# Twelve modulation chunks of the second layer computed by VectorE instead of TensorE

## The chip, the cores and the metric

The kernel runs on one core of a Trainium2 chip. The metric is the device time of one execution in microseconds (us); the time given for a kernel is the median of several runs. One more execution is recorded by the hardware profiler, and all rows of the trace come from it.

## The reference, cut to what matters

Two transformer blocks follow each other. The first has two layers on 256 context and 256 latent tokens; each layer scales and shifts its normalised input by six vectors of 1024 that come from one small condition, and ends in a gated feed-forward with a short convolution. The second block has two layers of its own and is not touched.

```python
mod_l = split(silu(c)     @ ada_w[l] + ada_b[l], 6)   # latent tokens
mod_c = split(silu(c_ctx) @ ada_w[l] + ada_b[l], 6)   # context tokens
hl = rms_norm(x_lat, norm_g[l, 0]) * (1 + mod_l[1]) + mod_l[0]
x_lat = x_lat + mod_l[2] * (mix_l @ w_out[l])
x_lat = x_lat + mod_l[5] * conv_ffn(modulate(x_lat, norm_g[l, 1], mod_l[3], mod_l[4]), ...)
```

The matrix `ada_w[l]` is 1024 x 6144 for each of two layers, and its product has only two rows (latent and context). It is handled in chunks of 256 columns: four chunks for each of the six vectors (types 0 to 5), 48 chunks in all.

## The kernel before, in words

Weights are streamed from HBM in blocks of 128 x 2048 floats (1 MB), in the order that `_plan` writes out. `wraw` issues each load on SP's queue into one of two `raw` buffers. A weight block is then split by `split` (lines 394 to 406) into two halves of 1024 columns, and each half into a high part (`whi`, a rounding copy on ScalarE, L401) and a low part (`wlo`, a subtraction on VectorE, L405). TensorE multiplies high by high, high by low and low by high (L444 to L446 in `mm_t`), so 48 matmuls of 512 columns make one block for 512 tokens.

A modulation chunk is another kind of entry in the same plan. It is not split: `ada` (line 534) multiplies the raw block with the activated condition `sc` in eight matmuls of 32 weight columns and 256 moving columns (L539; the trace shows 16 records for one chunk), ScalarE copies the result out (L545), and later, deferred by a cost, two transposes (L549), a reduction (L551) and an addition (L554) on VectorE put it into `mod`. The helper `spread` sets chunks between the weight blocks, one behind each, and keeps as many at the end as its third argument says.

The first feed-forward stage, `_ffn` with l = 0, runs over all 512 tokens in six parts of the hidden width. `up(i)` makes 22 blocks in all, gates and values: each result goes from PSUM through a convolution (ScalarE L1292, VectorE L1295 and L1296), a gate (L1304 to L1306) and a split of its own (L645, L649). `down(i - 1)` follows `up(i)` and adds 11 blocks into the stream `xt` (L1337). The results rotate through five PSUM buffers in this stage (`g` and `s`). The last `down` carries the normalisation of the next layer with it; then `flush_ada` handles chunks that stand at the end of the stage in the plan.

The order of the instructions on each engine is made by a scheduler of the framework, from the order in which the program writes them and from when their inputs and buffers come free. `_Pipe.tick` is called behind each group of matmuls with its cost and spaces out work that is interleaved, in units of columns times passes: a weight block of 48 matmuls of 512 columns counts 24576.

Of the kernel before, what the change touches and what calls it, by code (L numbers as in the profile page):

```python
# [10 lines left out]
F32 = mybir.dt.float32  # L11
F32R = mybir.dt.float32r
BF16 = mybir.dt.bfloat16
AF = mybir.ActivationFunctionType
ALU = mybir.AluOpType
# [13 lines left out]
C_ADAB = 0  # L29
C_NG = C_ADAB + 96  # L30
# [33 lines left out]
T_MB0 = 5440  # L64
T_MB1 = 5568
T_N = 5824

PERM = [16 * c + 4 * b + a for a in range(4) for b in range(4) for c in range(16)]

# [56 lines left out]
def _plan():  # L126
    p = []

    def cols(name, c0, cn=256, k0=0, kn=8, kind="g", at=0):
        p.append((kind, name, k0, kn, c0, cn, at))  # L130

    def ada(l, j, c):
        cols(("ada_w", l), 1024 * j + 256 * c, kind=("a", l, j, c))

    def adas(l, js):
        return [(l, j, c) for j in js for c in range(4)]

    def wout(l, half):
        for n in range(2):
            cols(("w_out", l), 512 * n, 512, 4 * half, 4, at=W_T if l else 0)  # L140

    def up(l, f0, fn):
        for s in range(fn // 2):
            cols(("ffn_up", l), 128 * f0 + 256 * s, at=W_T if l else 0)
            cols(("ffn_up", l), DFF + 128 * f0 + 256 * s, at=W_T if l else 0)

    def down(l, f0, fn):
        if fn == 4:
            cols(("ffn_down", l), 0, 512, f0, 4, at=W_T if l else 0)
            cols(("ffn_down", l), 512, 512, f0, 4, at=W_T if l else 0)  # L150
        else:
            cols(("ffn_down", l), 0, 1024, f0, 2, at=W_T if l else 0)

    def ffn(l):
        for i, fp in enumerate(FPARTS):
            up(l, *fp)
            if i:
                down(l, *FPARTS[i - 1])
        down(l, *FPARTS[-1])

    def spread(extra, start, tail=0, skip=0):
        q = list(extra)
        body = p[start:]
        del p[start:]
        for i, x in enumerate(body):
            p.append(x)
            if i >= skip and len(q) > tail:
                ada(*q.pop(0))
        while q:
            ada(*q.pop(0))  # L170

    e = ("even_w_in", 0)
    for c in range(4):
        if c == 3:
            cols(e, 512, 512, 4, 4)
        ada(0, 1, c)
        ada(0, 0, c)
        if c == 0:
            cols(e, 512, 512, 0, 4)
    n = len(p)  # L180
    for c0 in (2576, 2064, 2320, 0, 256, 1024, 1280):
        cols(e, c0, at=0 if c0 < 1024 else W_N)
    spread(adas(0, (2, 4)), n)
    n = len(p)
    cols(e, 1536)
    cols(e, 1792)
    wout(0, 1)
    wout(0, 0)
    a3, a5 = adas(0, (3,)), adas(0, (5,))
    spread(a3 + a5[:2], n, 1)  # L190
    n = len(p)
    late = adas(1, (2, 4, 3, 5))
    ffn(0)
    spread(a5[2:] + adas(1, (1, 0)) + late[:9], n, 1)
    o = ("odd_w_in", 0)
    n = len(p)
    for c0 in (512, 0, 256, 1280, 768, 1792, 1536, 1024, 2048):
        cols(o, c0, at=W_N)
    wout(1, 0)
    wout(1, 1)  # L200
    spread(late[9:16 - 1], n, 1, 3)
    n = len(p)
    ffn(1)
    spread(late[16 - 1:], n)
    a = ("a_w_in_2", 0)
    for hg in range(4):
        for g in range(3):
            for s in range(3):
                cols(a, 3072 * g + 1024 * s + 256 * hg, at=W_N)
        cols(a, 9216 + 256 * hg, at=W_T)  # L210
    for half in range(2):
        for n in range(2):
            cols(("a_w_out_2", 0), 512 * n, 512, 4 * half, 4, at=W_T)
    cols(("ple_w_proj_2", 0), 0, 1024, 0, 2, at=W_T)
    for n in range(4):
        cols(("ple_w_gate_2", 0), 256 * n, at=W_T)
    b = ("b_w_in_2", 0)
    cols(b, 1024, at=W_N)
    for hg in range(4):
        cols(b, 256 * hg, at=W_N)  # L220
        cols(b, 1280 + 256 * hg, at=W_T)
    for half in range(2):
        for n in range(2):
            cols(("b_w_out_2", 0), 512 * n, 512, 4 * half, 4, at=W_T)
    cols(("ple_w_proj_2", 1), 0, 1024, 0, 2, at=W_T)
    for n in range(4):
        cols(("ple_w_gate_2", 1), 256 * n, at=W_T)
    return p
# [8 lines left out]
class _Pipe:  # L237
    def __init__(self):
        self.pending, self.live = [], []
        self.pace = 1e9  # L240
        self.credit = 0.0
        self.later = []

    def defer(self, cost, fn):
        self.later.append([cost, fn])
# [26 lines left out]
            self.live.append(u)  # L272

    def tick(self, cost):
        if not self.pending and not self.live:
            return
        self.credit += cost
        if self.credit >= self.pace:
            self.credit = min(self.credit - self.pace, self.pace)
            self.slot()  # L280
# [29 lines left out]
class _K:  # L310
# [222 lines left out]
    def ada(self, kind, raw, now=False):  # L533
        nc = self.nc
        _, l, j, c = kind
        acc = self.po(128, 256) if now else self.pg(128, 256)
        for k in range(KD):
            g = 32 * (k % 4)
            nc.tensor.matmul(acc[g:g + 32], self.sc[:, k, :], raw[:, k], start=(k < 4), stop=(k >= 4))  # L539
        self.pipe.tick(2048)  # L540
        sb = self.e(256)
        if self.ada_vec:
            nc.vector.tensor_copy(sb, acc)
        else:
            nc.scalar.copy(sb, acc)  # L545
        def fin():
            tp = self.pt(128, 2, 128)
            for q in range(2):
                nc.tensor.transpose(tp[:, q], sb[:, 128 * q:128 * q + 128], self.ident)  # L549
            red = self.small([128, 2, 2], "adr")  # L550
            nc.vector.tensor_reduce(red, tp.rearrange("p q (g m) -> p q m g", g=4)[:, :, 0:2, :], axis=AX.X, op=ALU.add)  # L551
            o = self.mod[l][:, j, :, 2 * c:2 * c + 2].rearrange("p t q -> p q t")
            a0 = C_ADAB + 48 * l + 8 * j + 2 * c
            nc.vector.tensor_tensor(o, red, self.cols[:, a0:a0 + 2].unsqueeze(2).to_broadcast([128, 2, 2]), op=ALU.add)  # L554
            if j in (1, 4):
                g = C_NG + 16 * l + 8 * (j // 3) + 2 * c
                nc.vector.scalar_tensor_tensor(o, o, 1.0, self.cols[:, g:g + 2].unsqueeze(2).to_broadcast([128, 2, 2]),
                                               op0=ALU.add, op1=ALU.mult)

        if now:  # L560
            fin()
        else:
            self.pipe.defer(6000, fin)

    def stat(self, n):
        return [self.sa.tile([128, n], F32, tag=f"st{n}", name=self.nm("st")), n, 0]
# [707 lines left out]
def _ffn(K, l, segs, st, nxt=None):  # L1274
    nc, tc, cols = K.nc, K.tc, K.cols
    t0, n = segs[0][0], segs[-1][1] - segs[0][0]
    ns = n // 256
    with tc.tile_pool(name=f"f{l}", bufs=1, reuse_waits="tile") as pool, tc.tile_pool(name=f"fw{l}", bufs=3, reuse_waits="tile") as wx:
# [66 lines left out]
                         K.norm(st[0], l + 1, 0, segs[1], 256, 3) if st else ())  # L1345

        K.wide = True
        for i in range(len(FPARTS)):
            up(i)
            if i:  # L1350
                down(i - 1)
        K.lookahead = 0
        K.wide = False
        nst = nxt(segs) if nxt else None
# [596 lines left out]
def _layout(i):  # L1951
# [28 lines left out]
            w[n, :, 1024 * x:1024 * x + 1024] = src.reshape(ka, 128, cb).transpose(1, 0, 2).reshape(128, 1024)  # L1980
    out["w"] = w
    out["tab"] = _tables()
    return out


# [15 lines left out]
```

## Time and profile before

| | us |
|---|---|
| median of 3 runs | 1638.07 (1638.04 to 1639.7) |
| profiled execution, its own time | 1643.18 |
| span of the profiled execution | 1641.4 |
| TensorE busy (matmul) in the span | 1566.8 |
| VectorE busy | 1123.0 |
| ScalarE busy | 776.4 |
| GpSimd busy | 267.0 |

The span runs from the first to the last recorded instruction. PE is TensorE's matmul row, PEld its weight loads, DVE is VectorE, ACT is ScalarE, POOL is GpSimd, SP issues most of the loads. A wait is put down to the event that came last.

### The profile page before, as it was taken

How to read it: one execution, taken by the hardware profiler on the slowest of the kernel's cores; microseconds unless marked ns; L12 is line 12 of the kernel's file. 1: busy time of each engine (PE TensorE's matmuls, PEld its weight loads, DVE VectorE, ACT ScalarE, POOL GpSimd, SP SyncE). 2: the span in 40 equal slices, each digit the busy share in tenths (PEclk: the TensorE clock that was granted, in tenths of full speed). 3: DMA queues.
4: the chain of work that ended last, by engine and by line, in shares of the span. 5: the costliest groups of instructions: out<-in, count | busy, mean ns of one | idle time of the engine just before them, and what ended most of it. 6: DMA issues, size and time to landing. Idle time of an engine off the chain costs nothing.

```text
span 1641.4 us, 28309 instructions
## 1 busy us (share of the span) xinstructions
PE 1566.8 (95%) x11390; PEld 1374.0 (84%) x11390; DVE 1123.0 (68%) x2173; ACT 776.4 (47%) x1422; POOL 267.0 (16%) x239
## 2 busy tenths in 40 slices
PE   5989989999999999998999989999999999999998
PEld 3777767877777788878888889999989999989887
DVE  3676556675655566577677788677676767678896
ACT  3445464353333334234555465554455555455554
POOL 2321100030000000014231344441010101020111
PEclk9999999999999999999999999999999999999999
DMA  8232243344554532231333455554524343516232
GB/s 345 99 111 100 81 155 103 129 154 154 176 183 154 191 121 99 103 109 60 121 111 121 154 200 186 180 198 149 184 102 159 107 174 106 177 59 220 103 126 82
DMA packets 45107, 231.74 MB, mean 141 GB/s; under 512 B 12740, under 2 KB 15940, under 8 KB 18224
## 3 DMA queue, kind: packets, MB, share of 16 engines
q1 hardware_dynamic: 43776, 227.76, 40.0%
q10 hardware_dynamic: 1200, 2.17, 0.5%
q8 instruction: 90, 1.47, 0.4%
q14 instruction: 41, 0.34, 0.1%
HBM read 228.79 MB, written 1.12 MB: 140 GB/s over the span
## 4 chain that ended last, share of the span: by engine, by line
PE 75%; DVE 10%; POOL 4%; ACT 3%; DMA 2%; issue 2%; POOLq 0%; ACTq 0%; DVEq 0%; SPq 0%
PE g L444 10%; PE g L445 10%; PE g L446 10%; PE g L489 6%; PE g L491 6%; PE g L490 6%; PE s L444 4%; PE s L446 4%; PE s L445 4%; DVE wlo L405 3%; PE o L1049 3%; DMA raw<-in_w_dram 2%; PE t L1039 2%; PE g L539 2%; PE s L912 1%
## 5 line engine op out<-in xcount | busy, mean ns | idle before, releaser
L405 DVE TENSOR_TENSOR wlo<-raw,whi 128x1024 fp32r<-128x1024 f32 x289 | 358.6, 1252 | 180.6 <-ACT whi L401 179.9
L401 ACT CAST whi<-raw 128x1024 fp32r<-128x1024 f32 x322 | 332.6, 1048 | 312.4 <-DMA raw<-in_w_dram 123.7
L489 PE MATMUL g<-whi,H 128*128 128x256 f32 x1040 | 299.3, 288 | 4.3 <-ACT H L638 2.6
L491 PE MATMUL g<-whi,H 128*128 128x256 f32 x1040 | 295.7, 285 | 2.0 <-DVE H L640 1.0
L490 PE MATMUL g<-wlo,H 128*128 128x256 f32 x1040 | 293.8, 283 | 0.0
L444 PE MATMUL g<-H,whi 128*128 128x256 f32 (+1 forms) x872 | 274.0, 318 | 5.7 <-ACT H L1649 2.8
L445 PE MATMUL g<-H,whi 128*128 128x256 f32 (+1 forms) x872 | 273.3, 315 | 1.3 <-DVE H L1651 0.6
L446 PE MATMUL g<-H,wlo 128*128 128x256 f32 (+1 forms) x872 | 271.2, 312 | 0.0
L489 PEld LDWEIGHTS g<-whi,H 128*128 128x128 f32 x1040 | 198.5, 191 | 11.8 <-issue 4.6
L491 PEld LDWEIGHTS g<-whi,H 128*128 128x128 f32 x1040 | 198.1, 191 | 4.7 <-DVE H L640 3.0
L490 PEld LDWEIGHTS g<-wlo,H 128*128 128x128 f32 x1040 | 198.4, 191 | 0.5 <-issue 0.2
L444 PEld LDWEIGHTS g<-H,whi 128*128 128x128 f32 x872 | 163.7, 189 | 22.1 <-ACT H L1649 3.2
L445 PEld LDWEIGHTS g<-H,whi 128*128 128x128 f32 x872 | 164.9, 189 | 14.7 <-DVE H L640 1.8
L446 PEld LDWEIGHTS g<-H,wlo 128*128 128x128 f32 x872 | 165.0, 189 | 9.6
L1013 POOL TENSOR_SCALAR P<-P,rc 128x512 f32<-128x512 f32 (+2 forms) x64 | 54.6, 854 | 492.4 <-DVE rc L1811 258.7
L403 POOL TENSOR_TENSOR wlo<-raw,whi 128x1024 fp32r<-128x1024 f32 x33 | 81.1, 2457 | 105.7 <-ACT whi L401 104.5
L446 PE MATMUL s<-H,wlo 128*128 128x256 f32 (+1 forms) x264 | 88.1, 334 | 1.8 <-DVE wlo L405 1.8
L444 PE MATMUL s<-H,whi 128*128 128x256 f32 (+1 forms) x264 | 89.3, 338 | 0.0
L445 PE MATMUL s<-H,whi 128*128 128x256 f32 (+1 forms) x264 | 87.9, 333 | 0.0
L444 PE MATMUL g<-G,whi 128*128 128x256 f32 (+1 forms) x240 | 79.1, 330 | 2.1 <-DVE e L1296 2.1
L446 PE MATMUL g<-G,wlo 128*128 128x256 f32 (+1 forms) x240 | 78.1, 326 | 0.0
L445 PE MATMUL g<-G,whi 128*128 128x256 f32 (+1 forms) x240 | 78.1, 325 | 0.0
(420 smaller groups left out, 3047.6 us busy)
## 6 DMA issues: line engine op xcount, KB each, us to landing
raw<-in_w_dram SPq DMA_DIRECT2D x209, 1024.0 KB, 4.8
xt<-in_xt_dram SPq DMA_DIRECT2D x4, 512.0 KB, 5.4
mrow<-Md ACTq DMA_DIRECT2D x8, 256.0 KB, 4.7
nab<-in_rpb_dram SPq DMA_DIRECT2D x16, 128.0 KB, 3.6
out_dram<-xt SPq DMA_DIRECT2D x4, 256.0 KB, 4.5
agw<-in_agw_dram SPq DMA_DIRECT2D x1, 512.0 KB, 13.8
mka<-in_tab_dram SPq DMA_DIRECT2D x1, 512.0 KB, 3.4
plr<-in_p_dram SPq DMA_DIRECT2D x2, 256.0 KB, 3.6
```

The costliest lines, as they stand in the source:

```text
L401: nc.scalar.copy(hi, raw)
L403: nc.gpsimd.tensor_tensor(lo, raw, hi.bitcast(F32), op=ALU.subtract)
L405: nc.vector.tensor_sub(lo, raw, hi.bitcast(F32))
L444: nc.tensor.matmul(out, hi[:, k, s], X[0][:, x], start=f, stop=False)
L445: nc.tensor.matmul(out, hi[:, k, s], X[1][:, x], start=False, stop=False)
L446: nc.tensor.matmul(out, lo[:, k, s], X[0][:, x], start=False, stop=l)
L489: nc.tensor.matmul(out, X[0][:, a + k, s], hi[:, k], start=f, stop=False)
L490: nc.tensor.matmul(out, X[0][:, a + k, s], lo[:, k], start=False, stop=False)
L491: nc.tensor.matmul(out, X[1][:, a + k, s], hi[:, k], start=False, stop=l)
L539: nc.tensor.matmul(acc[g:g + 32], self.sc[:, k, :], raw[:, k], start=(k < 4), stop=(k >= 4))
L1013: nc.gpsimd.tensor_scalar(P[1], P[1], rc[:, 1:2], 0.0, op0=ALU.mult, op1=ALU.add)
L1049: nc.tensor.matmul(o[64 * e:64 * e + 64], vv(e, b), u["T"][e][:, b], start=(b == 0), stop=(b == kb - 1))
```

## The change

Twelve chunks of layer 1 (types 1, 0 and 2, four each) leave the plan, and with it the stream of raw blocks. `vector_ada` computes them instead: the activated condition of both token kinds is spread over all partitions (`cb`, 128 x 2 x 1024), and a chunk of `ada_w`, transposed on the host (`v`), comes as two loads of 128 x 1024 in three buffers `ar`. For each of the 24 half chunks and each token kind, one `tensor_tensor_reduce` multiplies a row of weights by the condition and sums it, with the bias as the start value, straight into `mod`. The steps are taken from `tick`, one for each 15000 units of cost, in the stage `_ffn` with l = 0; what is left is done ahead of the last `down`. The order of the chunks that stay is changed so that seven of them stand behind the first seven weight blocks of the stage and none at its end.

```diff
+VECTOR = [(1, j, c) for j in (1, 0, 2) for c in range(4)]
+VPACE = 15000
@@ _plan
-    late = adas(1, (2, 4, 3, 5))
+    late = adas(1, (4, 3, 5))
     ffn(0)
-    spread(a5[2:] + adas(1, (1, 0)) + late[:9], n, 1)
+    spread(a5[2:] + late[:5], n)
...
-    spread(late[9:16 - 1], n, 1, 3)
+    spread(late[5:11], n, 1, 3)
     n = len(p)
     ffn(1)
-    spread(late[16 - 1:], n)
+    spread(late[11:], n)
@@ _Pipe
+        self.side = None
...
     def tick(self, cost):
+        if self.side:
+            self.side(cost)
@@ _K
+    def vector_ada(self, pool):
+
+        nc = self.nc
+        cb = pool.tile([128, 2, 1024], F32, name="cb")
+        nc.sync.dma_start(cb.rearrange("p t k -> p (t k)"), self.aps["cb"].partition_broadcast(128))
+        jobs = [(l, j, 2 * c + q, n, q) for n, (l, j, c) in enumerate(VECTOR) for q in range(2)]
+
+        def fetch(i):
+            t = pool.tile([128, 1024], F32, tag="ar", name=self.nm("ar"), bufs=3)
+            nc.sync.dma_start(t, self.aps["v"][jobs[i][3]][:, 1024 * jobs[i][4]:1024 * jobs[i][4] + 1024])
+            return t
+
+        tiles = [fetch(0), fetch(1)]
+        yield
+        for t in range(2):
+            for s in (slice(0, 512), slice(512, 1024)):
+                sg = self.e(512)
+                nc.scalar.activation(sg, cb[:, t, s], AF.Tanh, scale=0.5)
+                nc.vector.tensor_scalar(sg, sg, 0.5, 0.5, op0=ALU.mult, op1=ALU.add)
+                nc.vector.tensor_mul(cb[:, t, s], cb[:, t, s], sg)
+            yield
+        for i, (l, j, m, _, _) in enumerate(jobs):
+            raw = tiles.pop(0)
+            if i + 2 < len(jobs):
+                tiles.append(fetch(i + 2))
+            a0 = C_ADAB + 48 * l + 8 * j + m
+            out = self.mod[l][:, j, :, m:m + 1]
+            for t in range(2):
+                prod = raw if t else pool.tile([128, 1024], F32, tag="prod", name=self.nm("prod"), bufs=1)
+                nc.vector.tensor_tensor_reduce(prod, raw, cb[:, t], 1.0, self.cols[:, a0:a0 + 1], ALU.mult, ALU.add,
+                                               out[:, t])
+                if t and j in (1, 4):
+                    g = C_NG + 16 * l + 8 * (j // 3) + m
+                    nc.vector.tensor_scalar(out, out, 1.0, self.cols[:, g:g + 1], op0=ALU.add, op1=ALU.mult)
+                yield
+
+    def side_step(self, steps):
+        state = [0.0]
+
+        def step(cost):
+            state[0] += cost
+            if state[0] >= VPACE:
+                state[0] -= VPACE
+                next(steps, None)
+
+        return step
@@ _ffn
         K.wide = True
+        steps = None
+        if split:
+            steps = K.vector_ada(pool)
+            next(steps)
+            K.pipe.side = K.side_step(steps)
         for i in range(len(FPARTS)):
             up(i)
             if i:
                 down(i - 1)
+        K.pipe.side = None
+        for _ in steps or ():
+            pass
@@ _layout (host)
+    out["cb"] = np.concatenate([i["c"][0], i["c_ctx"]])
+    out["v"] = np.stack([...])
```

## Rows read from the trace of the kernel before

**Rows 1.** The page: busy time by engine, and the chain that ended last.
```profile
PE 1566.8 (95%) x11390; PEld 1374.0 (84%) x11390; DVE 1123.0 (68%) x2173; ACT 776.4 (47%) x1422; POOL 267.0 (16%) x239
...
PE 75%; DVE 10%; POOL 4%; ACT 3%; DMA 2%; issue 2%; POOLq 0%; ACTq 0%; DVEq 0%; SPq 0%
```

**Rows 2.** Windows: stretch, length, busy us (instructions) by engine, clock, DMA share, GB/s.
```profile
345.00:728.00 383.00, 382.60 (x1946) 306.04 (x1944) 236.96 (x386) 138.82 (x192) 5.97 (x9) 1.00 0.42 144
360.00:560.00 200.00, 200.00 (x1065) 153.66 (x1064) 114.72 (x188) 70.36 (x98) 0.00 (x0) 1.00 0.49 169
600.00:700.00 100.00, 100.00 (x443) 82.81 (x442) 60.09 (x84) 34.07 (x42) 0.00 (x0) 1.00 0.28 95
```

**Rows 3.** Windows, instructions of L539 alone, then of L549: matmuls, weight loads.
```profile
360.00:560.00 200.00, 17.13 (x256) 6.67 (x256) 1.00 0.49 169
...
360.00:560.00 200.00, 6.08 (x32) 4.43 (x32) 1.00 0.49 169
```

**Rows 4.** Timeline of TensorE around one chunk: start us, duration, line, operation.
```profile
449.43 0.39 PE L446 MATMUL s<-G,wlo 128*128 128x512 f32 x1
449.75 1.07 PE L539 MATMUL s<-raw,sc 128*32 128x256 f32 x16
450.75 0.50 PE L444 MATMUL g<-G,whi 128*128 128x512 f32 x1
```

**Rows 5.** Waits of TensorE's weight loads, 353 to 728 us: total, times, longest.
```profile
PEld g L444 <- ACT e L1292: 2.9, 7, 0.4
```

**Rows 6.** Timeline of TensorE where the stage ends; idle time before in brackets.
```profile
728.09 1.07 PE L539 MATMUL g<-raw,sc 128*32 128x256 f32 x16
...
731.74 0.39 PE L489 MATMUL g<-whi,H 128*128 128x256 f32 x1 [2.58 <-ACT H L638]
```

**Rows 7.** Windows behind the end of the stage; the third number from the right is the granted clock.
```profile
738.00:743.00 5.00, 5.00 (x25) 5.00 (x25) 2.57 (x12) 0.41 (x1) 1.17 (x3) 0.51 0.01 3
```

**Rows 8.** Groups of VectorE, 360 to 700 us: count, busy us, mean ns, idle before.
```profile
L405 DVE TENSOR_TENSOR wlo<-raw,whi 128x1024 fp32r<-128x1024 f32 x61 | 73.2, 1222 | 50.6 <-ACT whi L401 50.5
...
L1306 DVE TENSOR_TENSOR e<-e,e 128x512 f32<-128x512 f32 x22 | 15.2, 690 | 0.6
...
L1305 DVE SCALAR_TENSOR_TENSOR e<-e,e 128x512 f32<-128x512 f32 x22 | 15.0, 682 | 0.0
...
L1295 DVE SCALAR_TENSOR_TENSOR e<-g,hw,e 128x510 f32<-128x510 f32 x14 | 10.5, 747 | 7.6 <-ACT e L1292 7.6
...
L551 DVE TENSOR_REDUCE adr<-t 128x4 f32<-128x16 f32 x17 | 3.0, 174 | 17.9 <-PE t L549 17.5
L554 DVE TENSOR_TENSOR mod<-adr,cols 128x4 f32<-128x4 f32 x17 | 2.8, 164 | 0.4
```

**Rows 9.** Instructions of L1808, a `tensor_tensor_reduce` elsewhere: ns min/median/max, first and last start.
```profile
L1808 DVE CUSTOM_DVE_ANT_0 e<-s,mka x32: 674/686/693, 1193.7 to 1440.2; 128x512 f32<-128x512 f32 x32
L1808 DVE DVE_READ_ACCUMULATOR2_ANT nb<- x32: 77/83/85, 1194.3 to 1440.9; 128x1 f32 x32
```

**Rows 10.** Timelines of SP, ScalarE and TensorE early in the stage; then ScalarE later.
```profile
364.08 0.33 SPq L391 DMA_DIRECT2D raw<-in_w_dram  x1
...
368.98 2.00 ACT L401 CAST whi<-raw 128x1024 fp32r<-128x1024 f32 x2 [1.11 <-DMA raw<-in_w_dram]
...
376.35 0.50 PE L444 MATMUL g<-H,whi 128*128 128x512 f32 x1
...
628.03 1.06 ACT L401 CAST whi<-raw 128x1024 fp32r<-128x1024 f32 x1 [1.20 <-PE s L445]
```

**Rows 11.** Loads from 0 to 40 us (GB/s in slices, then one group), then from 280 to 400.
```profile
GB/s 0 8 91 305 356 221 340 369 352 385 414 422 410 418 442 442 401 406 447 438 414 434 426 442 401 442 426 442 164 41 8 164 393 434 401 434 434 311 434 385
...
raw<-in_w_dram SPq DMA_DIRECT2D x11, 1024.0 KB, 10.4
...
raw<-in_w_dram SPq DMA_DIRECT2D x16, 1024.0 KB, 4.9
```

**Rows 12.** Timelines of SP and ScalarE at the start of the stage.
```profile
332.88 0.33 SPq L391 DMA_DIRECT2D raw<-in_w_dram  x1
...
339.09 1.99 ACT L401 CAST whi<-raw 128x1024 fp32r<-128x1024 f32 x2
...
343.54 0.60 ACT L638 ACTIVATE H<-e,mod 128x256 fp32r<-128x256 f32 x1 [2.46 <-DVE e L632]
```

More of the change, by code (lines that the diff above doesn't have):

```diff
@@ L1982, in _layout @@
     out["tab"] = _tables()
+    out["cb"] = np.concatenate([i["c"][0], i["c_ctx"]])
+    out["v"] = np.stack([i["ada_w"][l][:, 1024 * j + 256 * c:1024 * j + 256 * c + 256].T.reshape(2, 128, 1024)
+                         .transpose(1, 0, 2).reshape(128, 2048) for l, j, c in VECTOR])
     return out
```

## The prediction

> **What bounds the kernel now.** I read the busy shares first, then the chain that ended last [rows 1]. TensorE is busy for 95% of the span and holds 75% of the chain, VectorE 10%. So time is saved where TensorE gets less to do, provided that nothing else comes late there. An average over the span doesn't say that for the stage that is changed, so the second view is the busy time by stretch [rows 2]: from 345 to 728 us, which is the first feed-forward stage, TensorE has 382.6 of 383 us and granted clock 1.00, VectorE 237.0, and GpSimd nearly nothing. A busy matmul row alone proves little, because the shown durations overlap. The count does: between 600 and 700 us, where no modulation chunk runs, 442 weight loads and their matmuls pass, one every 0.2262 us, and TensorE has no idle time. The waits of TensorE in the stage are a few microseconds in all, in pieces of 0.4 us [rows 5]. TensorE sets this stage, and the removed work lies in it.
>
> **What is removed from TensorE.** The plan of before has 19 chunks in this stage: 2 of layer 0, 16 of 1 (the three types that are moved, and type 4) and one of type 3. Eighteen stand between the 33 weight chunks, the last one behind the last down projection. The new plan leaves 7, all between the first weight chunks. So 11 vanish from the dense stretch and one from the end of the stage.
>
> Price of one chunk in the dense stretch, two ways. Between 360 and 560 us there are 1064 weight loads [rows 2]; 256 belong to chunks (16 records each, so 16 chunks) and 32 to their transposes [rows 3]. The other 776 at 0.2262 us make 175.5 us; the remaining 24.5 us over 16 chunks are 1.53 us each. Directly, the matmul before a chunk starts at 449.43 us and the one behind it at 450.75 [rows 4]: 1.32 us, less one matmul's 0.23, is 1.09 us, without the transposes that come later. I take 1.5, because the count holds everything that a chunk costs; the direct row is the lower bound. 11 x 1.5 = 16.5 us less (12.0 to 16.8).
>
> The twelfth chunk, at 728.09 us, lies where TensorE has nothing else: it ends at 729.16 and the next layer's first matmul starts at 731.74, held by the normalisation on VectorE and ScalarE [rows 6]. Without it TensorE idles 1.1 us longer and saves nothing. What could change is the clock: from 738 to 743 us it is granted at 0.51, so about 1.2 GHz, after that idle time [rows 7]. The longer pause can move that stretch. All 5 us at the lower level cost some 2.5 us over the higher one, so the bounds are +2.5 (as much again at the lower clock) and -1.5 (the chunk's own time after all); I take 0, since the pause is there already.
>
> **What is added to VectorE.** 12 chunks become 24 jobs of two multiply-and-sum instructions, 48 on 128x1024. No row shows that form with two inputs in SBUF. The nearest are the subtraction of 128x1024 at 1.222 us [rows 8] and the same instruction on 128x512 with one input in PSUM, 0.686 us and 0.083 us for reading the sum [rows 9]; a plain product of 128x512 takes 0.690 [rows 8], so the sum costs little. 48 x (1.222 + 0.083) = 62.6 us. The table of the activated condition adds 8 operations of 128x512, under 0.69 each: 5.5 us. The 12 old reductions and additions, 0.174 + 0.164 us [rows 8], go: 4.1 us less. Net +64 us, on 237 in a stage of some 367: 82% busy. The cover is VectorE's idle time, 40 of 100 us even in the densest stretch of up and down projections [rows 2]. An evacuation can stand behind one of the new instructions for 1.3 us; a chunk's accumulators are five PSUM buffers deep, and an up chunk fills two in 10.9 us, so I price it at 0, and at +3 if the cover is patchy. ScalarE loses 12 copies and gains four Tanh; it was busy for a third of the stage.
>
> The Trainium skill has a rule against this: "Vector Engine (DVE) Microarchitecture Reference", section 7, says that the scalar-tensor-tensor form with two SBUF sources that aren't bf16 runs at half throughput, since both read ports are taken and none is left for the accumulator. The trace doesn't bear it out for the plain form: the gating product with two fp32 sources takes 0.682 us for 512 elements against 0.690 for a plain product [rows 8]. With an accumulator no run here shows it. What it would do is the second rival.
>
> **Queues that the change is moved past.** The 24 loads of 512 KB and the 1 MB table go on SP's queue, in order with the weights. The bytes of the chunks are the same 12 MB as before. A load waits for its buffer, that is for the second product of the job three before it, and the weights behind it on SP wait too. How much they can wait is different in two parts of the stage. Where no chunks run, ScalarE splits a weight half when TensorE frees a buffer (628.03 us, released by a matmul), not when a load lands [rows 10]: weights are several half chunks ahead. Where chunks run, the two raw buffers are held by them: a weight load is issued at 364.08, its first split starts on landing at 368.98 and is over at about 371.2 with VectorE's part, and TensorE wants it at 376.35 [rows 10]. The slack is some 5 us. After the change that part is 7 chunks long instead of 18, and a 512 KB load in front costs it 1.2 to 2.5 us (half of the 2.4 at 434 GB/s, and half of 4.9) [rows 11]: within the slack, 0.
>
> At the entry three loads, 2 MB, go in front of the first weights. Alone a megabyte lands in 4.9 us; in the full queue of the kernel's start, in 10.4 [rows 11]. So the load issued at 332.88 us, whose split starts at 339.09, may be 5 to 10 us late, and behind that split on ScalarE stands the normalisation at 343.54 that feeds TensorE [rows 12]. The split takes 2 us, so it has 2.5 us of room: 0 to 8 us are lost, I take 2, as TensorE waits for the normalisation there anyway.
>
> **Sum.** -16.5 + 0 (end) + 0 (VectorE) + 0 (queue) + 2 (entry) = -14.5 us. The profiled execution took 1643.2 us (span 1641.4), 5.1 over the median of the three timed runs, 1638.07; none of the terms depends on that difference. 1643.2 - 14.5 = 1628.7 for a profiled run, and 1638.07 - 14.5 = 1623.5 for the median. The bounds: -16.8 - 1.5 = -18.3 gives 1619.8; -12 + 2.5 + 3 + 8 = +1.5 gives 1639.6 if everything goes badly together; the entry and VectorE alone at their bad ends, -16.5 + 8 + 3 = -5.5, give 1632.6.
>
> **Rivals.**
> *First: the weights stand behind VectorE in SP's queue (slower).* Place: the 7 chunks at the start of the stage, where the slack is 5 us. The new steps are 15000 cost units apart, against 24576 for a weight chunk of 10.9 us: one step each 6.7 us. If a load stands in SP's queue ahead of weights and its buffer comes free only one step later, the weights start 6.7 us late and 1.2 to 2.5 behind the transfer: 8 to 9 us, 3 to 4 beyond the slack, for each of 7 weight chunks, 21 to 28 us. Taking 24: 1638.07 - 14.5 + 24 = 1647.5. It decides once the delay is over 5 us. Against it: order on the queues follows readiness (weights are split several chunks early today), and VectorE has idle time for the products.
>
> *Second: the sum halves VectorE's rate.* The products take 2.45 us: 48 x 2.53 = 121 us, VectorE 354 of 367 us. Two up chunks, 21.8 us, hold 4 splits (4.9), 8 taps of the convolution (6.0) and 6 operations of gating and its low part (4.1), 15.0 us [rows 8], plus 3.3 products (one a step of 6.7 us), 8.3 us: 23.3, over TensorE's 21.8. Eleven such pairs give back 16.5 us: 1623.5 + 16.5 = 1640, no measurable change.
>
> *Third: the chunks were no load.* If the pieces of 0.4 us around them were all that TensorE could do anyway, for example because the evacuations set the pace, the stage stays as long: 1638. Against it: the matmul period is the same with and without chunks.
>
> **How the numbers follow.** The sum with its bounds gets 0.73, the first rival 0.11, the second 0.08, the third 0.08. Faster by over 0.2% (3.3 us, about what a measurement of this kernel can tell from no change): the forecast's 0.73 and a little of the second, 0.75; within 0.2%: the third, most of the second and the forecast's worst corner, 0.13; slower: the first and what of the second goes further, 0.12. The range, 1617.5 to 1638.5, takes 2 us below the best sum for order that shifts elsewhere, and above reaches just past the third rival, so that the second's and the first's 0.19 are left out.
>
> **What would show it.** Right: 12 groups of 16 narrow matmuls missing, the last weight chunk of the stage starting some 14 us earlier, TensorE at 0.226 us per matmul throughout, VectorE near 80% with products at 1.2 to 1.3 us. First rival: TensorE idle between 345 and 440 us, released by splits, and SP waiting for products. Second: products over 2 us and TensorE waiting for evacuations. Entry: a gap before 360 us and the table's landing time. Wrong altogether: no idle time in the stage, and time lost in a stage that the change does not touch.

## The result, and the profile after

The changed kernel takes 1623.66 us (1620.44 to 1626.03), the kernel before 1638.48 beside it (1638.04 to 1639.7). The ratio is 0.9899, with an interval of 0.9886 to 0.9912, so 14.4 to 18.7 us less; the two medians alone differ by 14.8 us, the ratio stands for 16.5. The forecast was 1623.5. The profiled execution of after took 1623.34 us (span 1621.6), that of before 1643.18, so this pair differs by 19.8 us. Executions of one program scatter by several us (before ran from 1635 to 1645 us in the comparisons below), so the readings that follow compare the stage itself and not the spans.

The page of after, busy time by engine, then the chain that ended last, then the new loads (KB each, us from issue to landing); it answers to [rows 1]:

```profile
PE 1548.0 (95%) x11174; PEld 1366.0 (84%) x11174; DVE 1173.7 (72%) x2257; ACT 774.9 (48%) x1414; POOL 266.6 (16%) x239
...
PE 74%; DVE 10%; ACT 4%; POOL 3%; DMA 3%; issue 2%; POOLq 0%; ACTq 0%; DVEq 0%; SPq 0%
...
ar<-in_v_dram SPq DMA_DIRECT2D x24, 512.0 KB, 4.5
...
cb<-in_cb_dram SPq DMA_DIRECT2D x1, 1024.0 KB, 5.5
```

TensorE has 18.8 us less busy time and VectorE 50.7 more, and yet the shares of the chain hardly move: TensorE still sets the time. Where the time went is seen by stage. From the first matmul of the feed-forward stage to the first matmul of the next layer, before takes 332.96 to 731.74 us, which is 398.78, and after 332.30 to 715.16, which is 382.86: 15.9 us less. The two first matmuls of the stage, before and then after:

```profile
332.96 0.50 PE L444 MATMUL g<-H,whi 128*128 128x256 f32 x2
...
332.30 0.50 PE L450 MATMUL g<-H,whi 128*128 128x256 f32 x2
```

The next layer and its feed-forward stage are 391.66 and 388.64 us long, the second block 518.0 and 517.8. The 3.0 us in the next layer are no more than one code scatters there from trace to trace (386.4 to 390.4 us in this kernel and the four runs below with the same code in that layer and no chunk at the end of the stage). So the gain that stands clear of scatter lies in the stage that was changed.

Windows of after through that stage, as in [rows 2] (stretch, length, then busy us and instructions of PE, PEld, DVE, ACT, POOL, granted clock, DMA share, GB/s):

```profile
345.00:360.00 15.00, 14.82 (x82) 12.54 (x81) 14.08 (x27) 9.28 (x15) 4.33 (x5) 1.00 0.41 156
360.00:400.00 40.00, 40.00 (x223) 30.05 (x222) 38.80 (x71) 17.53 (x25) 0.00 (x0) 1.00 0.68 237
400.00:440.00 40.00, 39.47 (x195) 30.25 (x194) 38.18 (x64) 16.90 (x24) 0.00 (x0) 1.00 0.75 264
440.00:480.00 40.00, 40.00 (x178) 33.12 (x177) 39.43 (x60) 14.20 (x17) 0.00 (x0) 1.00 0.59 200
480.00:520.00 40.00, 40.00 (x178) 33.13 (x177) 39.77 (x64) 15.88 (x20) 0.00 (x0) 1.00 0.43 154
520.00:560.00 40.00, 40.00 (x178) 33.13 (x177) 25.42 (x34) 13.82 (x17) 0.00 (x0) 1.00 0.31 105
560.00:700.00 140.00, 140.00 (x626) 116.22 (x625) 84.00 (x126) 44.09 (x55) 0.00 (x0) 1.00 0.30 99
```

Read the DVE column first. From 360 to 520 us VectorE is busy for 156.2 of 160 us, 98%, where before it had 115 of 200 [rows 2]; behind 520 us it falls back to 60%. The new work was not spread over the stage at 82%, as its pacing by cost would have it: it was done at the first chance. Then the PE column: TensorE loses 0.5 us in the slice from 400 to 440 us and nothing afterwards. From 440 us on, 177 weight loads pass in each 40 us, one every 0.226 us, the same as in the stretch of before without chunks.

The instructions of the tile `ar` (ns min/median/max, first and last start):

```profile
L600 DVE CUSTOM_DVE_ANT_0 prod<-ar,cb,cols x24: 1270/1278/1284, 357.6 to 521.0; 128x1024 f32<-128x1024 f32 x24
```

VectorE's groups from 345 to 714 us (count, busy us, mean ns, idle before), as in [rows 8]:

```profile
L411 DVE TENSOR_TENSOR wlo<-raw,whi 128x1024 fp32r<-128x1024 f32 x68 | 82.7, 1220 | 35.5 <-ACT whi L407 35.4
...
L600 DVE DVE_READ_ACCUMULATOR2_ANT mod<- 128x1 f32 x48 | 3.9, 81 | 0.0
```

One product has a record of 1.278 us, and reading its sum one of 0.081. Records of neighbours overlap, so these two don't simply add. VectorE's timeline (start, duration):

```profile
392.95 1.28 DVE L600 CUSTOM_DVE_ANT_0 prod<-ar,cb,cols 128x1024 f32<-128x1024 f32 x1
394.16 0.08 DVE L600 DVE_READ_ACCUMULATOR2_ANT mod<- 128x1 f32 x1
394.16 0.68 DVE L702 TENSOR_TENSOR G<-e,G 128x512 fp32r<-128x512 f32 x1
```

The next instruction starts 1.21 us after the product did, together with the read of the sum. Where VectorE doesn't wait, this distance is 1.20 to 1.33 us, mostly 1.2, so the 48 take some 58 us, between 357.6 and 524 us.

What TensorE waits for from 353 to 712 us (total, times, longest), and what SP's queue waits for from 330 to 540:

```profile
PEld g L452 <- DVE wlo L411: 1.3, 3, 0.5
...
SPq L397 <- DVE wlo L411: 89.1, 17, 13.0
SPq L580 <- DVE mod L600: 56.2, 18, 8.2
```

SP does stand behind the products: 18 waits, up to 8.2 us. TensorE's weight loads wait 1.3 us in all for low parts. The first rival's queue is there, and its cost isn't.

### The profile page after: what moved, and what is told of

It is laid out like the page before. It is cut to its first block, busy times and chain, and to the rows that moved or that the text cites. A ratio compares the mean times of both kernels' runs of the same rounds, so it can differ in the third digit from the quotient of the medians.

```text
span 1621.6 us, 27974 instructions
## 1 busy us (share of the span) xinstructions
PE 1548.0 (95%) x11174; PEld 1366.0 (84%) x11174; DVE 1173.7 (72%) x2257; ACT 774.9 (48%) x1414; POOL 266.6 (16%) x239
## 4 chain that ended last, share of the span: by engine, by line
PE 74%; DVE 10%; ACT 4%; POOL 3%; DMA 3%; issue 2%; POOLq 0%; ACTq 0%; DVEq 0%; SPq 0%
PE g L450 10%; PE g L452 10%; PE g L451 10%; PE g L495 6%; PE g L497 6%; PE g L496 6%; PE s L450 4%; PE s L451 4%; PE s L452 4%; DVE wlo L411 3%; PE o L1102 3%; DMA raw<-in_w_dram 2%; PE t L1092 2%; PE g L545 1%; PE s L965 1%
## 5 line engine op out<-in xcount | busy, mean ns | idle before, releaser
L450 PE MATMUL g<-H,whi 128*128 128x256 f32 (+1 forms) x856 | 267.2, 315 | 5.1 <-ACT H L1710 2.7
L451 PE MATMUL g<-H,whi 128*128 128x256 f32 (+1 forms) x856 | 266.7, 313 | 1.0 <-DVE H L1712 0.3
L452 PE MATMUL g<-H,wlo 128*128 128x256 f32 (+1 forms) x856 | 264.9, 311 | 2.4 <-DVE wlo L411 2.4
L450 PEld LDWEIGHTS g<-H,whi 128*128 128x128 f32 x856 | 161.0, 189 | 19.1 <-ACT H L1710 3.1
L451 PEld LDWEIGHTS g<-H,whi 128*128 128x128 f32 x856 | 161.7, 189 | 13.1 <-DVE H L693 1.5
L450 PE MATMUL s<-H,whi 128*128 128x512 f32 (+1 forms) x280 | 95.1, 340 | 1.1 <-ACT H L691 1.1
L451 PE MATMUL s<-H,whi 128*128 128x512 f32 (+1 forms) x280 | 94.9, 339 | 0.0
L452 PE MATMUL s<-H,wlo 128*128 128x512 f32 (+1 forms) x280 | 94.3, 337 | 0.0
```

The costliest lines, as they stand in the source:

```text
L450: nc.tensor.matmul(out, hi[:, k, s], X[0][:, x], start=f, stop=False)
L451: nc.tensor.matmul(out, hi[:, k, s], X[1][:, x], start=False, stop=False)
L452: nc.tensor.matmul(out, lo[:, k, s], X[0][:, x], start=False, stop=l)
```

## The experiments

The theory: TensorE sets the stage, a chunk among the weights costs it 1.5 us, and VectorE's added work and loads are covered as long as the weights have a lead. Against it stand three others. The weights are held behind the products in SP's queue, and a part of the gain is lost by it. VectorE, at 98%, is itself near to setting the pace. And the chunk at the end of the stage was no free one. Each run is compared with the kernel before on the same chip.

**The twelve chunks computed by nobody.** The loads, the table and the products go, `mod` gets a constant in their place.

```diff
-            steps = K.vector_ada(pool)
-            next(steps)
-            K.pipe.side = K.side_step(steps)
+            nc.vector.memset(K.mod[1][:, 0:3], 0.5)
```

> The twelve chunks are left out of the plan and nobody computes them (the modulation they stand for is set to 0.5): the changed kernel without VectorE's part, its loads and its table. Theory (TensorE sets the stage and VectorE's part is hidden): the same as the changed kernel within 2 us, 1622 to 1624, as nothing but a small cost at the entry goes. Rival (VectorE's part and its loads give back part of the gain, through SP's queue or the evacuations): 5 us or more below the changed kernel, under 1619.

Measured: 1620.23 us (1619.19 to 1625.77), ratio 0.9889 (0.9869 to 0.9908). The stage takes 382.3 us, against 382.86 with VectorE's work. One window, 440 to 480 us:

```profile
440.00:480.00 40.00, 40.00 (x178) 33.14 (x177) 24.40 (x36) 11.36 (x13) 0.00 (x0) 1.00 0.34 116
```

The same 178 matmuls pass with VectorE at 61% here as with 99% in after. All that was added costs the stage 0.6 us, which is no more than scatter: the same code ahead of the stage ends between 330.4 and 333.0 us in the eleven traces. The time of the whole execution doesn't tell the two kernels apart, as the intervals overlap. What is left of the gain is then the removal of the chunks.

**One chunk back at the end of the stage.** It is one of the seven that stay, moved from among the weights.

```diff
-    spread(a5[2:] + late[:5], n)
+    spread(a5[2:] + late[:5], n, 1)
```

> The changed kernel with one of its seven remaining chunks put back to the end of the stage, behind the last down projection. Theory (a chunk there lies where TensorE waits anyway, and one fewer in the dense stretch saves 1.5 us): 1 to 2 us below the changed kernel, with the idle time before the next layer's first matmul shorter by 1 us and that matmul at the same distance from the last down projection. Rival (a chunk costs the same wherever it is): no difference, and the first matmul 1 us later after the last down projection.

Measured: 1623.67 us (1621.81 to 1627.3), ratio 0.9904 (0.9887 to 0.9921). The stage is 380.73 us, 2.1 shorter, about what a chunk costs. The gain of 1 to 2 us that was expected doesn't arrive: the next layer and its feed-forward stage take 393.8 us, 5.2 more. Part of that can be scatter (386.4 to 390.4 us in five traces of that code without the chunk). The head of that layer shows where 2.5 of these may begin. TensorE, this kernel, then after (start, duration, idle before):

```profile
707.51 1.07 PE L545 MATMUL g<-raw,sc 128*32 128x256 f32 x16
...
711.16 0.39 PE L495 MATMUL g<-whi,H 128*128 128x256 f32 x1 [2.58 <-ACT H L691]
...
718.32 0.85 PE L638 MATMUL t<-cmean,st 128*128 128x2 f32 x4
...
720.46 1.05 PE L644 MATMUL t<-ident,nrs 128*128 128x128 f32 x4
```

```profile
714.72 0.58 PE L638 MATMUL t<-cmean,st 128*128 128x2 f32 x4 [3.37 <-DVE st L631]
715.16 0.36 PE L495 MATMUL g<-whi,H 128*128 128x256 f32 x1
...
721.96 1.23 PE L644 MATMUL t<-ident,nrs 128*128 128x128 f32 x4 [0.55 <-POOL nrs L656]
```

L638 is the sum for the second half of the normalisation, and L644 spreads its result. With a chunk at the end, L638 stands behind the first weight block, and L644 comes 9.3 us after the first matmul. Without one, L638 is ahead of the first matmul and L644 comes 6.8 us after it. In the kernel before, whose stage ends in a chunk, the two are at 738.90 and 741.04, and the first matmul at 731.74 [rows 6]: 9.3 us again. It is 9.3 in all three kernels of this study with a chunk there, and 6.4 to 7.8 in the eight without. So the chunk at the end moved work of the next layer to a later place.

**The products made twice.** The first pair of each half chunk is made two more times and its results are overwritten, so VectorE has 96 of them.

```diff
+                if not t:
+                    nc.vector.tensor_tensor_reduce(prod, raw, cb[:, 1], 1.0, ..., out[:, 0])
+                    nc.vector.tensor_tensor_reduce(prod, raw, cb[:, 1], 1.0, ..., out[:, 1])
```

> Every product of the table with a half chunk is made twice: 96 multiply-and-sum instructions of about 1.36 us instead of 48, 65 us more on VectorE, the result unchanged. In the changed kernel VectorE is busy for 97 to 99% from 360 to 523 us and TensorE has no idle time there. Theory (evacuations and splits keep their precedence, the products only fill VectorE's gaps and run on into the rest of the stage, where 40% of VectorE is free): the same time within 3 us, VectorE saturated until about 700 us. Rival (VectorE's idle time is the limit; with it full, evacuations come late): over 1633, TensorE waiting for VectorE or ScalarE in the stage.

Measured: 1628.96 us (1625.64 to 1630.01), ratio 0.9928 (0.9913 to 0.9944), by the ratios some 5 us over after. The stage is 386.4 us, 3.5 longer, and the loss has one place. Windows:

```profile
360.00:400.00 40.00, 36.66 (x190) 27.54 (x189) 37.76 (x66) 16.71 (x24) 0.00 (x0) 0.96 0.55 196
...
600.00:640.00 40.00, 40.00 (x178) 33.10 (x178) 39.95 (x60) 17.07 (x22) 0.00 (x0) 1.00 0.42 147
```

TensorE's waits in the first of them (total, times, longest), which are one and the same chunk:

```profile
PEld s L545 <- DVE e L1354: 2.9, 1, 2.9
...
PE s L545 <- DMA raw<-in_w_dram: 2.7, 1, 2.7
```

From 400 to 640 us VectorE is at 96 to 100% and TensorE has 40 of 40 us in every slice. A full VectorE is therefore not what costs in that stretch: what TensorE needs from it still came in time. The price, some 2 us above the 3 that the theory allowed, is paid from 360 to 400 us, where chunks still stand among the weights and one of them waits for its load; the granted clock behind that wait, 0.96 in this window against 1.00 in after, is a part of it. Whether the load was late by the `raw` buffers or by SP's queue this run doesn't separate.

**One load ahead, two buffers.** The weights stand in SP's queue behind a load whose buffer comes free a job later.

```diff
-            t = pool.tile([128, 1024], F32, tag="ar", name=self.nm("ar"), bufs=3)
+            t = pool.tile([128, 1024], F32, tag="ar", name=self.nm("ar"), bufs=2)
-        tiles = [fetch(0), fetch(1)]
+        tiles = [fetch(0)]
-            if i + 2 < len(jobs):
-                tiles.append(fetch(i + 2))
+            if i + 1 < len(jobs):
+                tiles.append(fetch(i + 1))
```

> Two buffers for the half chunks instead of three, and only one load ahead: each load on SP's queue waits for the products of the job just before, with the weights queued behind it. Theory (the weights are split far enough ahead that a wait on SP doesn't reach TensorE): the same within 2 us, with longer waits of SP for the products. Rival (SP's order is what the part with chunks lives on): 1630 or more, TensorE idle between 345 and 440 us, released by splits.

Measured: 1627.62 us (1624.83 to 1631.97), ratio 0.9925 (0.9908 to 0.9943), by the ratios some 4 us over after, with intervals that just touch; the stage is 388.5 us, 5.7 longer. The window of the loss:

```profile
360.00:400.00 40.00, 36.40 (x182) 26.96 (x181) 35.58 (x63) 13.53 (x21) 0.00 (x0) 0.91 0.62 222
```

A row of TensorE's timeline in it:

```profile
368.13 1.03 PE L545 MATMUL s<-raw,sc 128*32 128x256 f32 x2 [3.60 <-DMA raw<-in_w_dram]
```

And a wait of the weight loads there:

```profile
PEld s L545 <- DVE wlo L411: 3.9, 1, 3.9
```

That is the first rival's mechanism, in the place that it named: a chunk among the first weight blocks, idle for 3.6 us until its load has landed. But it happens once or twice and then the weights have their lead; it costs 4 to 6 us and not 21 to 28. Not all of that is the wait: the granted clock behind it is 0.50 from 368 to 372 us, and 0.91 over the window, where after has 1.00. With three buffers, as the change has them, TensorE has no idle time in this window, and 0.5 us in the next.

**VectorE's work without the removal.** The plan of before stays, with all its chunks, and VectorE computes the twelve as well. Both write `mod`, and a vector that is scaled in place is scaled twice, so the values aren't the reference's; the work is all there.

```diff
-    late = adas(1, (4, 3, 5))
+    late = adas(1, (2, 4, 3, 5))
-    spread(a5[2:] + late[:5], n)
+    spread(a5[2:] + adas(1, (1, 0)) + late[:9], n, 1)
...
```

> The kernel before with all of its chunks on TensorE, and VectorE makes the products, the table and the loads of the changed kernel as well (both write the same values). Theory (what is added is hidden): the same as the kernel before, within 3 us; the weights have little room in the part with chunks, which now lasts the whole first half of the stage, so a loss of up to 4 us may show, in pieces that a late weight or chunk load releases. Rival (the loads compete with the chunks' own, 24 MB instead of 12, on one queue): 8 us or more above the kernel before.

Measured: 1645.44 us (1640.52 to 1648.76), ratio 1.0022 (1.0009 to 1.0035): 3.6 us slower than before. The stage is 404.31 us, 5.5 longer. Two windows:

```profile
440.00:480.00 40.00, 38.71 (x205) 29.55 (x204) 35.65 (x62) 9.09 (x12) 0.00 (x0) 1.00 0.71 246
480.00:520.00 40.00, 37.46 (x195) 27.61 (x194) 33.51 (x54) 14.24 (x21) 0.00 (x0) 1.00 0.64 220
```

A row of TensorE's timeline in the first:

```profile
451.49 0.50 PE L450 MATMUL g<-G,whi 128*128 128x512 f32 x1 [1.04 <-ACT whi L407]
```

TensorE is late from 440 to 520 us, where chunks still stand in the stream, and waits for splits, while VectorE is at 84 to 89%, less than in after. So the same work on VectorE costs the stage 0.6 us with 7 chunks in the stream and 5.5 with 18. The reading is that taking the chunks out does two things at once: it takes their time from TensorE, and it gives the weights the lead that covers the rest. This run has twice the chunk bytes on SP's queue too, and it doesn't show which of the two makes the splits late; the rate in these windows, 246 and 220 GB/s, is below the 264 at which after loses 0.5 us.

**The kernel before, without the chunk at its end.** That chunk goes among the weights; nothing else is touched.

```diff
-    spread(a5[2:] + adas(1, (1, 0)) + late[:9], n, 1)
+    spread(a5[2:] + adas(1, (1, 0)) + late[:9], n)
```

> The kernel before with its last chunk of the stage moved from behind the last down projection into the dense stretch; nothing else. In the traces of the changed kernel and of the one with a chunk put back, the second broadcast of the next layer's normalisation comes 6.8 and 9.3 us after that layer's first matmul. Theory (a chunk at the end pushes the second statistics matmul behind the first block of the next layer): that distance falls from 9.3 to some 7 us, the stage grows by 1.5 us for the 19th chunk, the next layer's head shrinks by 2.5: 0 to 2 us below the kernel before. Rival (the head got shorter for another reason, such as earlier weights): distance unchanged at 9.3, time 1 to 2 us longer.

Measured: 1641.88 us (1637.43 to 1645.65), ratio 1.0004 (0.9992 to 1.0016). TensorE at the end of the stage:

```profile
732.37 0.99 PE L585 MATMUL t<-cmean,st 128*128 128x2 f32 x4 [3.37 <-DVE st L578]
...
733.22 0.56 PE L489 MATMUL g<-whi,H 128*128 128x256 f32 x1
...
739.62 1.22 PE L591 MATMUL t<-ident,nrs 128*128 128x128 f32 x4 [0.55 <-POOL nrs L603]
```

The next layer's first matmul is 1.5 us later than in before, about the price of a chunk among the weights (the stage, which begins earlier here, is 400.91 us, 2.1 longer), and the sum (L585) now stands ahead of it. Its result is spread 6.4 us behind that matmul, where before it took 9.3: 1.4 us earlier in absolute time. The order follows the chunk at the end here as well. The time shows no difference, and the order isn't all that differs: the granted clock was lower in this run. The 20 us from the next layer's first matmul, in before, in after and in this run (length, busy us and instructions of PE, PEld, DVE, ACT, POOL, then the granted clock):

```profile
731.74:751.74 20.00, 18.80 (x101) 16.65 (x102) 15.22 (x42) 10.00 (x19) 15.14 (x19) 0.74 0.22 88
...
715.16:735.16 20.00, 18.21 (x105) 16.44 (x105) 14.81 (x40) 10.07 (x19) 15.92 (x19) 0.74 0.12 48
...
733.22:753.22 20.00, 18.48 (x102) 17.14 (x103) 14.41 (x39) 9.49 (x18) 15.28 (x19) 0.69 0.11 45
```

Over 20 us that is some 1.0 us more at the lower clock. So one chunk more among the weights, an earlier sum and a lower clock nearly cancel; what each is worth alone this run doesn't show.

**All 24 chunks of the second layer, then the same begun later.** The first puts everything that layer 1 has on VectorE; the second begins that work behind the first `up`. The pace is raised, so that all steps fit.

```diff
-VECTOR = [(1, j, c) for j in (1, 0, 2) for c in range(4)]
-VPACE = 15000
+VECTOR = [(1, j, c) for j in (1, 0, 2, 4, 3, 5) for c in range(4)]
+VPACE = 7500
-    late = adas(1, (4, 3, 5))
-    spread(a5[2:] + late[:5], n)
+    spread(a5[2:], n)
...
```

> All 24 chunks of layer 1 go to VectorE in the first feed-forward stage, twice as many products at half the spacing; only the 2 chunks of layer 0 stay between the weights there, and none in the next layer. Theory (TensorE sets these stages, a chunk costs it 1.5 us in the dense stretch, VectorE's gaps hold 130 us of products): 5 x 1.5 = 7.5 us less in the stage, 6 to 9 us less for 7 chunks in the next layer, 1607 to 1612, with VectorE saturated until about 690 us. Rival (the products run past the end of the stage, in front of the next layer's normalisation): 1620 or more, with TensorE idle for over 5 us before the next layer's first matmul.

Measured: 1615.21 us (1613.16 to 1617.34), ratio 0.9837 (0.982 to 0.9855), above the 1607 to 1612 expected. Five chunks fewer make 7.5 us; the stage is 379.24 us, only 3.6 shorter than after. The second block, which is not touched, takes 527.2 us in this trace, 9.4 more than in after. The next run has the same plan and 518.0 there, so the plan alone doesn't make it; all five executions here are slow, at 1613 us or more, and the cause stays open. The window in which the stage loses:

```profile
360.00:400.00 40.00, 37.70 (x159) 30.22 (x158) 38.98 (x61) 19.71 (x27) 0.00 (x0) 0.96 0.60 210
```

Two rows of TensorE's timeline:

```profile
357.29 0.50 PE L448 MATMUL s<-H,wlo 128*128 128x512 f32 x1 [1.08 <-DVE wlo L407]
...
366.05 0.80 PE L446 MATMUL s<-H,whi 128*128 128x512 f32 x1 [1.03 <-ACT whi L403]
```

And the products, as above:

```profile
L596 DVE CUSTOM_DVE_ANT_0 prod<-ar,cb,cols x48: 1273/1284/1300, 354.8 to 657.9; 128x1024 f32<-128x1024 f32 x48
```

The products begin at 354.8 us, and TensorE waits mostly for splits, some 3.4 us from 345 to 400; a granted clock of 0.96 over 40 us costs up to 1.6 us more. With two chunks left in the stream their hold on the buffers is unlikely to be the reason. What is left is the start: weights and products begin together, before any weight is split ahead. The next edit tests that.

```diff
-        if split:
-            steps = K.vector_ada(pool)
-            next(steps)
-            K.pipe.side = K.side_step(steps)
...
+            if split and not i:
+                steps = K.vector_ada(pool)
+                next(steps)
+                K.pipe.side = K.side_step(steps)
```

> As the run with all 24 chunks on VectorE, but the loads, the table and the products begin behind the first part of the up projections (four weight blocks later), with the steps closer together. In the run before, TensorE lost some 3.5 us between 345 and 400 us, released by splits that came late, and 9 us more than the changed kernel in the second block. Theory (products that begin before the weights have a lead cost the 3.5 us): TensorE without idle time from 360 us on, the stage 3 to 4 us shorter than in that run. Rival (one queue and a full VectorE cost it wherever they begin): the same loss a few blocks later. If the second block is slow again, the loss there belongs to the order that follows from the shorter plan; if it isn't, to that execution. 1608 to 1612, or 1615.

Measured: 1607.38 us (1605.3 to 1612.19), ratio 0.9806 (0.9785 to 0.9826). The pace is 6500 here, so the steps come closer together too; a late start at the pace of 7500 was not run. This is the fastest kernel of the study, ahead of before and after. Windows:

```profile
360.00:400.00 40.00, 40.00 (x190) 32.35 (x188) 35.42 (x51) 22.72 (x31) 0.00 (x0) 1.00 0.50 180
...
560.00:600.00 40.00, 40.00 (x178) 33.11 (x177) 40.00 (x69) 11.22 (x14) 0.00 (x0) 1.00 0.52 174
```

And its products:

```profile
L596 DVE CUSTOM_DVE_ANT_0 prod<-ar,cb,cols x48: 1270/1278/1285, 393.9 to 669.1; 128x1024 f32<-128x1024 f32 x48
```

The products begin 39 us later, TensorE has 40 of 40 us in every slice from 360 to 680, with VectorE at 95 to 100% from 400 on, and the stage takes 374.2 us: 5.0 less than the early start, about the 3.4 and up to 1.6 us above, and 8.7 less than after, for 5 chunks fewer. The next layer and its feed-forward stage, which lose 7 chunks, take 381.8, 6.9 less than after. The 7.8 us between the medians of the two kernels are not these 5.0 alone: in their traces the next layer is 3.5 us longer in the late one and the second block 9.2 shorter.

**The changed kernel, begun later.** The edit is the same, with the twelve chunks and a pace of 13000.

> The changed kernel with its loads, table and products begun behind the first part of the up projections. Theory (the loads at the entry cost next to nothing, since the normalisation sets the pace there): the same as the changed kernel within 1.5 us, and the first weight split after the chunk loads at about 339 us again instead of 345.5. Rival (the three loads in front of the weights cost the entry 2 us or more): 2 to 4 us below the changed kernel.

Measured: 1623.0 us (1618.95 to 1625.04), ratio 0.9897 (0.9881 to 0.9913), no difference from after; the stage is 382.1 us. TensorE has no idle time from 360 to 680. ScalarE's first split in its timeline:

```profile
343.94 1.03 ACT L407 CAST whi<-raw 128x1024 fp32r<-128x1024 f32 x1
```

And the products:

```profile
L600 DVE CUSTOM_DVE_ANT_0 prod<-ar,cb,cols x24: 1272/1278/1285, 394.5 to 554.3; 128x1024 f32<-128x1024 f32 x24
```

The late start gains nothing with twelve chunks, as all that was added had cost the stage only 0.6 us. The first split did not come back to 339 us as expected: the scheduler issued the table's load at 328.8 us and the first loads of half chunks at 333.2 us all the same. Only the products moved, so this run doesn't test what the loads at the entry cost.

## Why the prediction was right, and where not

**Dense chunks: right.** Eleven at 1.53 us make 16.8; the stage became 15.9 us shorter, and 16.15 if it is counted to the split that ScalarE starts behind the last down projection (728.08 us in before, 711.27 in after). The rest fits too: 33 blocks of 48 matmuls at 0.2262 us are 358.3 us, and 18 chunks at 1.53 leave 12.9 us of the 398.78 for the two ends, 7 leave 13.9 of the 382.86. So the count from the matmuls' spacing [rows 2, 3] was the price. The direct row, 1.09 us [rows 4], gives 12.0 and would have been 4 us too low.

**The end chunk: 0 holds as far as the time shows, a side effect was missed.** The step had it save nothing, with only the clock open. From before to after the clock did not move: it was granted at 0.51 behind the end of the stage [rows 7] and at 0.50 in after, about 1.2 GHz both times, and at 0.74 in the mean of 20 us in both. What the step did not see is that the chunk settled the order of the next layer's first instructions. Without it the second half of the normalisation comes 2.5 us sooner after the first matmul. The eleven kernels show that order; they don't show that 2.5 us arrive at the end. With the chunk moved alone, in the kernel before, the time did not change (0.9992 to 1.0016).

**The entry: the load's delay was right, its price was not.** The first split moved from 339.09 [rows 12] to 345.50 us, 6.4 late, within the 5 to 10 foreseen. TensorE did not pay the 2 us: from 330 to 360 us it is busy for 28.97 us in after, for 27.89 in before and for 27.88 in the run without the new loads. The normalisation went ahead of the split. ScalarE in after:

```profile
341.86 1.59 ACT L691 ACTIVATE H<-e,mod 128x256 fp32r<-128x256 f32 x3 [3.37 <-DVE e L685]
345.50 1.04 ACT L407 CAST whi<-raw 128x1024 fp32r<-128x1024 f32 x1
```

In before it stood behind that split, at 343.54, and ScalarE waited there for VectorE and not for the split (2.46 us idle [rows 12]). The step kept the order of before and took a late load for a late engine.

**VectorE: 0 was near, the picture wrong.** The pacing did not spread the products; they were done at the first chance, and VectorE stood at 98% for 160 us. The 82% hold only as a mean: it was busy for 280 of 355 us from 345 to 700 us, 79%. It cost TensorE 0.5 us, and the kernel with 96 products shows why: with VectorE full to 640 us, TensorE still lost nothing behind 400. One product with its read took mostly 1.2 us from start to start, not 1.305, and VectorE's busy time grew by 50.7 us, not by 64.

**The queue: right for three buffers.** The first rival gave 21 to 28 us. Its mechanism is real, but it was counted for each of 7 chunks, and it ends after one or two: 4 to 6 us with two buffers, 3.5 to 5 with the products doubled, 0.6 as the change was made. That the lead of the weights ends it is the reading that fits all runs; no run measures the lead itself.

**The second rival** needed products of 2.45 us, and they take 1.278. The rule beside it, in the Trainium skill's "Vector Engine (DVE) Microarchitecture Reference", section 7, halves the throughput of the scalar-tensor-tensor form with two SBUF sources that aren't bf16. The row of the products shows no half rate: two fp32 sources in SBUF with a sum, 1024 elements, take 5% more than the plain subtraction of the same size (1.220 us). But the profile calls the instruction CUSTOM_DVE_ANT_0 and not SCALAR_TENSOR_TENSOR, so the rule's own form with a sum was not run. **The third rival**, that chunks were no load, fell with the run that leaves them out: without anything in their place the stage shrinks by 16.5 us.

**The sum.** Forecast -14.5; in the stage it was -15.9, that is -16.8 for the chunks and +0.9 left over for the two ends and VectorE together. The 2 us at the entry were the term that was too large. The measured 14.4 to 18.7 us hold both, so the near agreement of the medians is in part luck.

## What to carry to other kernels

Price work that is to be taken off the bounding engine from the spacing of its instructions in a stretch with that work and in one without; the gap around a single one left out over a quarter of it here. Work that is moved to another engine was covered here even with that engine at 98%, with few chunks left in the stream and except at the start of the stage, so begin it behind that start: this was worth 5 us of stage time with 24 chunks, and nothing with twelve. And look at what the last item of a stage does to the order of the next one before calling it free, even if its price could not be told from scatter here.

## What the runs showed of the hardware that was not expected

A load of 512 KB landed 4.5 us after its issue in this stage, and one of 1 MB in the same stretch of after (345 to 530 us) took 5.7, so half the bytes were not half the time:

```profile
raw<-in_w_dram SPq DMA_DIRECT2D x24, 1024.0 KB, 5.7
```

In before such a load takes 4.9 [rows 11], so the weights' own loads became 0.8 us slower; the prediction had taken 1.2 to 2.5. A multiply-and-sum of 128x1024 floats from two tiles in SBUF has a record of 1.278 us, but the next instruction starts 1.21 us after it, and the read of its sum, 0.081 us, runs beside that one. One wait of TensorE of 3.6 us cost more than itself: the clock behind it was granted at 0.50 from 368 to 372 us. And in the late run with 24 chunks VectorE was busy for 95 to 100% of 280 us without a TensorE that reads its results being late.
